# Two token streams staggered by half a tile at four layer norms of a two-layer flow backbone, and the adaLN vectors moved out of those norms

## The chip, the cores and the metric

The kernel runs on one core of a Trainium2 chip. The metric is the device time of one launch in microseconds (us), the median of several runs. TensorE (PE), VectorE (DVE), ScalarE (ACT) and GpSimd (POOL) each have a queue of instructions that they take in order; SyncE (SP) issues the DMA transfers.

## What is computed

The model has two layers over 512 tokens: 256 latent tokens and 256 context tokens, in 1024 channels. The two streams have the same weights and different adaLN vectors. Everything is fp32.

```python
for l in range(DEPTH):                       # DEPTH = 2
    mod = split(silu(c) @ ada_w[l] + ada_b[l], 9)        # latent; modc from c_ctx for the context
    h  = macaron_ffn(h,  mod[0],  mod[1],  mod[2],  ...) # hc likewise
    y, yc = token_mixer(modulate(h, mod[3], mod[4]), modulate(hc, modc[3], modc[4]), ...)
    h  = layer_norm(alpha * h + mod[5] * y)
    h  = macaron_ffn(h,  mod[6],  mod[7],  mod[8],  ...)
    # the last layer drops the context after the mixer
def macaron_ffn(h, shift, scale, gate, w_in, w_out, g, b):
    a, b = split(modulate(h, shift, scale) @ w_in, 2)
    return layer_norm(alpha * h + 0.5 * gate * ((silu(a) * b) @ w_out))
```

The mixer runs three branches (a gated recurrence, a long convolution, windowed attention), merges them with gates and applies one output projection. So there are six layer norms: after the FFN, the mixer and the FFN of each layer.

## The kernel before, in words

Channels lie on the 128 partitions, tokens along the free dimension: a tile is 128 channels by 512 tokens (latent 0 to 255, context 256 to 511). In the second layer the context is dropped behind the mixer's projections, so that later tiles have 256 tokens. Each weight is loaded in fp32 by SP into `raw` (`wload`, L120 to 132), split by ScalarE into a high part (L130) and by VectorE into the low rest (L132). A product is three matmuls in fp32r: high by high, high by low, low by high (`mm3`, L139 to 143; `projO`, L523 to 536). An FFN (`ffn`, L466) goes twice through eleven input blocks of two products (SwiGLU in `finish`, L474) and eight output products of eleven blocks each (L508 to 518), each added to the residual tile `ah` (`residual`, L361 to 380), which also sums the tiles and their squares for the norm. The mixer's output projection (L1132 to 1136) does the same with eight products.

`norm` (L391 to 455) then takes column sums with one-column matmuls (`token_mean`, L388 and 389), the mean over all partitions (L423), the variance (L424, L425), rstd by a pow on GpSimd (L426), spreads it over partitions (`bcast`, L457 to 462), and makes the eight operands of the next sub-layer: centre (L411), scale (L438), affine and cast (`mod`, L341 to 353), low part (`low`, L355 to 358). GpSimd writes the scaled residual back (L449). Its TensorE part is in a fixed order, behind the last product.

The adaLN vectors come in 18 groups of 512 columns a layer. They are made in three ways: the first four of layer 0 at the start; `ada_group` (L286 to 297) on TensorE, eight products of two stream columns by 512, in four column tiles, then four transposes and a sum; and `ada_pairs` (L250 to 284), which multiplies on VectorE (L266) weight by weight, for two groups and two streams a pair, and reduces on TensorE (L273). The latter is a generator: `pull` (L171 to 175) advances it by `BG` = (2, 1) steps behind each input block and each output product of an FFN, except in the first three slots. `run` (L1172 to 1194) says what goes where: three `ada_group`s inside each of the norms 0 to 3 (`HOLES` sets how many steps go between the norm's matmuls) and two in the fifth, four more in FFN slots (`fill`), and seven pairs (`bg`).

The order on each engine is made by a scheduler at build time, by program order and readiness; inside a `manual_schedule` block the named engines keep the written order, and `issue_after` puts an instruction behind another one. `U`, `T`, `E`, `H` and so on are pools of 128x512 slabs (`SLABS`), and `pj`, `ph`, `pa` are three, two and three PSUM banks (`BANKS`).

Of the kernel before, what the change touches and what calls it, by code (L numbers as in the profile page):

```python
# [27 lines left out]
PAIR0 = ((6, 7), (8, 9), (13, 14))  # L28
HOLES = (3, 0, 0, 2)
BG = (2, 1)  # L30
LAG = 4
SKIP = (1, 2, 3)
# [45 lines left out]
class Net:  # L78
    def __init__(self, ctx, tc, a, out):
        self.tc, self.nc, self.a, self.out = tc, tc.nc, a, out  # L80
        self.uid = 0
        self.now, self.chains = 0.0, []
        ep = lambda **k: ctx.enter_context(tc.tile_pool(**k))
# [50 lines left out]

    def split(self, src, hi, lo):
        self.nc.scalar.activation(hi, src, AF.Copy)
        self.nc.vector.tensor_tensor(lo, src, hi, ALU.subtract)
# [32 lines left out]

    def pull(self, n):  # L171
        self.slot += 1
        if self.slot not in self.bg_skip:
            for _ in range(n):
                next(self.bg, None)
# [74 lines left out]
    def ada_pairs(self, l, gs, mods):  # L250


        nc = self.nc
        for pair in gs:
            acc = []
            for g in pair:
                acc += [self.slab("W", name="acc") for _ in range(2)]
                for k in range(KD):
                    w = self.slab("EH"[k % 2], name="adaw")
                    nc.sync.dma_start(out=w, in_=self.a["ada_w"][l, g, k])  # L260
                    for t, s in zip(acc[-2:], range(2)):
# [5 lines left out]
                    if k % 2:  # L267
# [12 lines left out]
            v = tr.rearrange("p (b g s x) -> p g b s x", b=4, g=2, s=2)  # L280
            for i, g in enumerate(pair):
                bias = self.par("ada_b", l * 72 + g * 4, 4)
                nc.vector.tensor_tensor(mods[:, g * 4:g * 4 + 4, :], v[:, i, :, :, 0],
                                        bias.unsqueeze(2).to_broadcast([P, 4, 2]), ALU.add)
# [106 lines left out]
    def norm(self, l, i, ah, TT, st, mods_next, ish, keep=True, out=None, fill=()):  # L391
        nc = self.nc
        nb = TT // P
        units, end = [], None
        for f in fill:
            x = self.ada_group(*f)
            units += [(x, 1), end, (x, 1), (x, 1), (x, 1)] if end else [(x, 1)] * 4
            end = (x, 0)
        units += [end] if end else []

        def more(n):
            while units and n >= units[0][1]:
                x, m = units.pop(0)
                next(x, None)
                n -= m
# [8 lines left out]
        with self.tc.manual_schedule(engines={mybir.EngineType.PE}), self.tc.issue_after(self.last_mm.ins):  # L414
            more(HOLES[0])
            for tb in range(nb):
                self.token_mean(st["stat"][:, tb:tb + 1], st["s1"], tb, False, False)
            more(HOLES[1])
            for tb in range(nb):
                self.token_mean(st["stat"][:, 4 + tb:5 + tb], st["sq"], tb, False, tb == nb - 1)  # L420
            more(HOLES[2])
# [7 lines left out]
            more(HOLES[3])  # L429
            R = self.bcast(rstd, nb, "pa")  # L430
            more(100)
# [23 lines left out]
        return u + [self.low(x, TT) for x in pend]  # L455
# [10 lines left out]
    def ffn(self, l, i, u, ah, TT, gate, extra=None, pre=None):  # L466
# [4 lines left out]
        for half in range(2):  # L471
            g = []

            def finish(pa, pb):  # L474
                s = self.slab("T", name="silu")
                nc.scalar.activation(s[:, :TT], pa[:, :TT], AF.Silu)  # L476
                nc.vector.tensor_tensor(s[:, :TT], s[:, :TT], pb[:, :TT], ALU.mult)  # L477
                gh, gl = self.hilo(GTAGS[len(g)], "g")
                self.split(s[:, :TT], gh[:, :TT], gl[:, :TT])
                g.append((gh, gl))  # L480

            j = 0
            while j < HALF:
# [5 lines left out]
                if n == 3:  # L489
                    banks = self.projO(pre, u, [TT] * 6)  # L490
                elif n == 2:
                    banks = self.projO([w(q) for q in range(3)], u, [TT] * 3)
                    finish(*banks[:2])
                    banks = banks[2:] + self.projO([w(3)], u, [TT], "ph")
# [5 lines left out]
                self.pull(BG[0])  # L500
# [7 lines left out]
            for d in range(KD):  # L508
                if half and d == KD - 1:
                    self.squares(st, TT)  # L510
# [8 lines left out]
                self.pull(BG[1])  # L519
# [45 lines left out]
    def hgrn_proj(self, l, h, u, NQ, outer):  # L565
        nc = self.nc
        i = 4 + 4 * h
        if outer:
            ws = [self.wload(self.a["mix_w"][l, i + q], tags=(None, "QQ", "FF")[q],
                             marks=self.marks if q in PIN else None) for q in range(3)]  # L570
            pz = self.projO(ws, u, (T, T, NQ))
        else:
            pz = [self.projT(l, i + r, u, T) for r in range(2)]
        f, k = self.wide("F", name="f"), self.wide("F", name="k")
        for r in range(2):
            col = l * 8 + r * 4 + h
            c = slice(r * T, (r + 1) * T)
            nc.scalar.activation(f[:, c], pz[r], AF.Sigmoid)
            nc.scalar.activation(k[:, c], pz[r], AF.Sigmoid, scale=-1.0)
# [3 lines left out]
        pq = pz[2] if outer else self.projT(l, i + 2, u, NQ)  # L583
        q = self.slab("S", name="q")
        nc.scalar.activation(q[:, :NQ], pq[:, :NQ], AF.Copy)
        pg = self.projT(l, i + 3, u, NQ, "ph" if outer else "pj")
# [477 lines left out]
    def mixer(self, l, u, ah, TT, gate):  # L1064
# [31 lines left out]
        def proj(h):  # L1096
            hp.append(self.hgrn_proj(l, h, u, TT, h == 0))
# [34 lines left out]
        for d in range(KD):  # L1132
            if d == KD - 1:
                self.squares(st, TT)
# [4 lines left out]
    def run(self):  # L1139
# [21 lines left out]
        for d in range(KD):  # L1161
# [7 lines left out]
            if d < 2:  # L1169
# [4 lines left out]
                    [self.tables_b, lz(ada, 0, 15), lz(self.filters, 1)],  # L1174
            (1, 0): [None] + [lz(ada, 1, 15)],
        }
        bg = {(0, 0): self.ada_pairs(0, PAIR0, mods[0]),
              (0, 1): self.ada_pairs(1, [(1, 2), (3, 7)], mods[1]),
              (1, 0): self.ada_pairs(1, [(8, 9), (13, 14)], mods[1])}
        for l in range(DEPTH):  # L1180
            TT = T if l < DEPTH - 1 else L
            self.bg, self.slot, self.bg_skip = bg.get((l, 0), iter(())), 0, SKIP
            st = self.ffn(l, 0, u, ah, T, lambda: self.mod_cols(mods[l], 2), fill.get((l, 0)), pre if l == 0 else None)
            u = self.norm(l, 0, ah, T, st, mods[l], 3, fill=[(l, g, mods[l]) for g in (10, 11, 12)])
            st = self.mixer(l, u, ah, TT, self.mod_cols(mods[l], 5))
            u = self.norm(l, 1, ah, TT, st, mods[l], 6,
                          fill=[(l, 16, mods[l]), (l, 17, mods[l])] + ([(l + 1, 0, mods[l + 1])] if l < DEPTH - 1 else []))
            self.bg, self.slot, self.bg_skip = bg.get((l, 1), iter(())), 0, SKIP
            st = self.ffn(l, 1, u, ah, TT, lambda: self.mod_cols(mods[l], 8), fill.get((l, 1)))
            if l < DEPTH - 1:  # L1190
                u = self.norm(l, 2, ah, TT, st, mods[l + 1], 0, fill=[(l + 1, g, mods[l + 1]) for g in (4, 5, 6)])
            else:
                self.norm(l, 2, ah, TT, st, None, 0, out=self.out)
# [127 lines left out]
```

## Time and profile before

| | |
|---|---|
| median of 3 runs | 2384.67 us (2384.52 to 2386.96) |
| the profiled execution | 2383.82 us, span 2382.0 us |
| granted TensorE clock, mean | 0.994 |
| busy share: TensorE, its weight loads | 98%, 83% |
| busy share: VectorE, ScalarE, GpSimd | 60%, 41%, 7% |
| DMA | 360.41 MB, 151 GB/s |

The busy time of an engine counts whatever its instructions are for, so TensorE's 98% includes the column sums and adaLN products between sub-layers. A row of a timeline has the start, the busy time, engine, line, operation, the tiles written and read, the shape and the number of instructions merged; idle time before it, with what ended it, stands in brackets. An fp32 product appears as two records. A matmul's own time includes its way through the array, so the pace is read from starts.

### The profile page before, as it was taken

What the parts mean: (1) busy time and instruction counts of PE and PEld (TensorE: products, weight loads), DVE (VectorE), ACT (ScalarE), POOL (GpSimd) and SP (SyncE); (2) the same over time, 40 slices, a digit from 0 to 9 for tenths busy, and PEclk for the clock granted to TensorE, in tenths of its full rate; (3) what the DMA queues carried; (4) which work ended last, traced back from release to release, by engine and by line L of the source; (5) the groups of instructions that cost most, each with busy time, mean ns of one, the idle gap of its engine ahead of it and who ended that gap; (6) DMA issues with size and microseconds to landing.
All of it is one profiled execution on the core that took longest, in us unless ns stands there. A gap on an engine that the chain in (4) does not pass through costs nothing.

```text
span 2382.0 us, 34116 instructions
## 1 busy us (share of the span) xinstructions
PE 2343.4 (98%) x13112; PEld 1971.4 (83%) x13112; DVE 1440.5 (60%) x2403; ACT 970.3 (41%) x1663; POOL 170.3 (7%) x158
## 2 busy tenths in 40 slices
PE   8999999999999999999999999999999999999998
PEld 4778778699888888867888877878887999998998
DVE  3647848656877665776433357363346687776555
ACT  3424324444654433343222234222225466645443
POOL 1003002210010000010000001000002111000000
PEclk9999999999999999999999999999999999999999
DMA  9435734723223445765332247243224344694564
GB/s 365 139 102 172 233 97 121 263 67 105 77 80 128 154 137 190 254 207 156 108 121 93 83 139 251 90 149 106 92 86 137 118 129 138 197 320 153 171 198 125
DMA packets 153314, 360.41 MB, mean 151 GB/s; under 512 B 16576, under 2 KB 38208, under 8 KB 153152
## 3 DMA queue, kind: packets, MB, share of 16 engines
q1 hardware_dynamic: 153152, 358.24, 46.2%
q8 instruction: 103, 1.69, 0.3%
q14 instruction: 59, 0.48, 0.1%
HBM read 331.96 MB, written 26.21 MB: 150 GB/s over the span
## 4 chain that ended last, share of the span: by engine, by line
PE 94%; DMA 2%; DVE 2%; ACT 1%; issue 1%; SPq 1%; POOL 0%; ACTq 0%; DVEq 0%
PE pj L530 18%; PE pj L531 18%; PE pj L533 18%; PE pj L141 7%; PE pj L143 7%; PE pj L142 7%; PE ph L632 2%; PE pj L551 1%; PE pj L552 1%; PE pj L553 1%; PE ph L293 1%; PE pa L1006 1%; PE pa L873 1%; PE ph L678 1%; PE pa L997 1%
## 5 line engine op out<-in xcount | busy, mean ns | idle before, releaser
L132 DVE TENSOR_TENSOR lo<-raw,hi 128x1024 fp32r<-128x1024 f32 (+1 forms) x455 | 524.6, 1154 | 451.1 <-ACT hi L130 450.2
L530 PE MATMUL pj<-uh,hi 128*128 128x512 f32 (+1 forms) x2096 | 752.5, 359 | 4.6 <-ACT uh L352 3.0
L533 PE MATMUL pj<-ul,hi 128*128 128x512 f32 (+1 forms) x2096 | 749.2, 358 | 1.1 <-DVE ul L357 1.1
L531 PE MATMUL pj<-uh,lo 128*128 128x512 f32 (+1 forms) x2096 | 749.5, 358 | 0.0
L130 ACT ACTIVATE hi<-raw 128x1024 fp32r<-128x1024 f32 (+1 forms) x455 | 446.4, 982 | 602.3 <-issue 251.2
L530 PEld LDWEIGHTS pj<-uh,hi 128*128 128x128 f32 x2096 | 396.6, 189 | 74.5 <-issue 8.6
L533 PEld LDWEIGHTS pj<-ul,hi 128*128 128x128 f32 x2096 | 396.1, 189 | 59.3 <-DVE ul L357 2.5
L531 PEld LDWEIGHTS pj<-uh,lo 128*128 128x128 f32 x2096 | 396.4, 189 | 56.8 <-issue 2.1
L142 PE MATMUL pj<-g,hi 128*128 128x512 f32 (+1 forms) x704 | 255.7, 363 | 0.0
L143 PE MATMUL pj<-g,lo 128*128 128x512 f32 (+1 forms) x704 | 255.5, 363 | 0.0
L141 PE MATMUL pj<-g,hi 128*128 128x512 f32 (+1 forms) x704 | 255.4, 364 | 0.0
L141 PEld LDWEIGHTS pj<-g,hi 128*128 128x128 f32 x704 | 132.8, 189 | 23.7 <-issue 1.7
L143 PEld LDWEIGHTS pj<-g,lo 128*128 128x128 f32 x704 | 132.9, 189 | 22.3 <-DVE ah L366 1.7
L142 PEld LDWEIGHTS pj<-g,hi 128*128 128x128 f32 x704 | 132.9, 189 | 21.3 <-issue 0.8
L476 ACT ACTIVATE silu<-pj 128x512 f32<-128x512 f32 (+1 forms) x87 | 47.3, 543 | 244.2 <-PE pj L533 244.2
L266 DVE SCALAR_TENSOR_TENSOR acc<-adaw,sc,acc 128x512 f32<-128x512 f32 x196 | 138.2, 747 | 3.9 <-DMA adaw<-ada_w 3.5
L477 DVE TENSOR_TENSOR silu<-silu,pj 128x512 f32<-128x512 f32 (+1 forms) x83 | 51.3, 619 | 147.0 <-PE pj L533 135.7
L366 DVE SCALAR_TENSOR_TENSOR ah<-pj,hg,ah 128x256 f32<-128x256 f32 x136 | 60.3, 478 | 90.0 <-PE pj L143 70.3
L426 POOL TENSOR_TENSOR rstd<-var,mhalf 128x4 f32<-128x4 f32 (+1 forms) x6 | 6.4, 1063 | 1111.9 <-DVE var L425 1111.9
L551 PE MATMUL pj<-hi,uh 128*128 128x256 f32 x288 | 82.2, 288 | 0.2
L552 PE MATMUL pj<-lo,uh 128*128 128x256 f32 x288 | 81.9, 286 | 0.0
L553 PE MATMUL pj<-hi,ul 128*128 128x256 f32 x288 | 81.6, 286 | 0.0
(293 smaller groups left out, 3110.3 us busy)
## 6 DMA issues: line engine op xcount, KB each, us to landing
raw<-ffn_in SPq DMA_DIRECT2D x176, 512.0 KB, 3.4
adaw<-ada_w SPq DMA_DIRECT2D x256, 256.0 KB, 4.8
raw<-mix_w SPq DMA_DIRECT2D x124, 512.0 KB, 3.5
raw<-ffn_out SPq DMA_DIRECT2D x64, 384.0 KB, 3.1
raw<-ffn_out SPq DMA_DIRECT2D x64, 320.0 KB, 2.9
raw<-branch_w SPq DMA_DIRECT2D x24, 512.0 KB, 5.3
adaw<-ada_f SPq DMA_DIRECT2D x32, 256.0 KB, 6.0
raw<-out_w SPq DMA_DIRECT2D x16, 512.0 KB, 4.6
```

What stands on the lines that cost most here:

```text
L130: nc.scalar.activation(hi[:, :n], raw[:, :n], AF.Copy)
L132: nc.vector.tensor_tensor(lo[:, :n], raw[:, :n], hi[:, :n], ALU.subtract)
L141: nc.tensor.matmul(out, lhsT=wh, rhs=xh, start=start, stop=False)
L142: nc.tensor.matmul(out, lhsT=wh, rhs=xl, start=False, stop=False)
L143: self.last_mm = nc.tensor.matmul(out, lhsT=wl, rhs=xh, start=False, stop=stop)
L266: nc.vector.scalar_tensor_tensor(t, w, c, t, ALU.mult, ALU.add)
L530: self.nc.tensor.matmul(p, lhsT=hi, rhs=u[k][0][:, :n], start=(k == 0), stop=False)
L531: self.nc.tensor.matmul(p, lhsT=lo, rhs=u[k][0][:, :n], start=False, stop=False)
L533: self.last_mm = self.nc.tensor.matmul(p, lhsT=hi, rhs=u[k][1][:, :n], start=False, stop=(k == KD - 1))
L551: nc.tensor.matmul(o, lhsT=u[k][0][:, s], rhs=hi[:, c], start=(k == 0), stop=False)
L552: nc.tensor.matmul(o, lhsT=u[k][0][:, s], rhs=lo[:, c], start=False, stop=False)
L553: nc.tensor.matmul(o, lhsT=u[k][1][:, s], rhs=hi[:, c], start=False, stop=(k == KD - 1))
```

## The change

At norms 0, 1, 2 and 3 (both FFNs and the mixer of layer 0, and the first FFN of layer 1), `norm` gives way to `seam`. The last two output products of an FFN, or the last three of the mixer, are computed for the latent stream first and then for the context stream, in products of 256 columns; the latent stream's statistics, centring and rstd stand among the context stream's matmuls. Then the first three products of the next sub-layer run for the latent stream, with the context stream's statistics and centring among them, and then for the context stream. TensorE, VectorE and ScalarE all keep the written order in this block. The weights of those output products are split into slabs `U` (`wlast`); the fourth product of the next sub-layer follows with 512 columns.

The adaLN groups of those norms move: 10 and 11 of layer 0 into the first FFN's slots, 16 and 17 into the second's, 14 of layer 1 beside 15 into the third's; the others into `ada_pairs`, which has four parts in the first FFN, three in the second and three in the third (the last of them with four groups for the latent stream alone). `PULL` = (2.0, 1.0) replaces `BG`; in the second half an output product pulls one more, in the first half of the first FFN a half more. The filters of layer 1 move from the first FFN to the second. In the fifth norm the order of column sums and adaLN steps changes, and the groups' ends move behind the first products.

```diff
-PAIR0 = ((6, 7), (8, 9), (13, 14))
-HOLES = (3, 0, 0, 2)
-BG = (2, 1)
-SKIP = (1, 2, 3)
+SKIP = 3
+PULL = (2.0, 1.0)
+STATS = 5
+SEAM = {mybir.EngineType.PE, mybir.EngineType.DVE, mybir.EngineType.Activation}
...
+    def seam(self, l, prods, gate, ah, st, i, mods, ish, ws, ns):
...
+        def stats(s):
+            stat = self.pbank("pa")
+            x3 = (st["s2"], st["sq"][s], st["s1"])
+            for n, (x, o) in enumerate(zip(x3, (2, 2, 0))):
+                for tb in range(2):
+                    self.token_mean(stat[:, o + tb:o + tb + 1], x, (0 if n == 1 else 2 * s) + tb, n == 0 and tb == 0,
+                                    n == 2 and tb == 1)
+            mean[s] = self.pbank("pa")
+            nc.tensor.matmul(mean[s][:, :L], lhsT=self.onesD, rhs=st["s1"][:, cols(s)], start=True, stop=True)
...
+            nc.gpsimd.tensor_tensor(rstd[s][:, :2], var[:, :2], self.mhalf[:, :2], ALU.pow)
...
+        def operand(d, s):
...
+            nc.vector.tensor_tensor(t, t, R[s][:, :L], ALU.mult)
+            if d:
+                nc.scalar.activation(x[:, :L], t, AF.Identity, bias=b, scale=g)
+                h = nc.scalar.activation(uh[:, c], x[:, :L], AF.Copy)
...
+            w = nc.vector.tensor_tensor(ul[:, c], x[:, :L], uh[:, c], ALU.subtract)
...
+        with self.tc.manual_schedule(engines=SEAM), self.tc.issue_after(self.last_mm.ins):
+            banks = []
+            for s in range(2):
+                n = 0
+                for d, ops in prods:
+                    p = self.pbank("pj")
+                    for k, (wh, wl, xh, xl) in enumerate(ops):
+                        self.mm3(p[:, :L], wh, wl, xh[:, cols(s)], xl[:, cols(s)], k == 0, k == len(ops) - 1)
+                        n += s
+                        if n == STATS:
+                            stats(0)
+                        elif STATS < n <= STATS + KD:
+                            center(n - STATS - 1, 0)
+                        elif n == STATS + KD + 1:
+                            R[0] = self.bcast(rstd[0], 2, "pa")
+                    if not s or d < KD - 1:
+                        self.residual_of(d, p, gate, ah, st, s)
+                last = p
+            for s in range(2):
+                w = ws[:ns[s]]
...
+                for k in range(KD):
+                    if k < KD - 1:
+                        next(x[k + 1])
+                    next(x[k])
...
+                    if not s:
+                        if k == 0:
+                            self.residual_of(KD - 1, last, gate, ah, st, 1)
+                        elif k == 2:
+                            stats(1)
+                        elif 2 < k < KD - 1:
+                            center(2 * k - 6, 1)
+                            center(2 * k - 5, 1)
+                        if k == 5:
+                            R[1] = self.bcast(rstd[1], 2, "pa")
...
-                self.pull(BG[1])
+                if d == 3 and half:
+                    for _ in self.bg:
+                        pass
+                elif d < 3 or not half:
+                    self.pull(PULL[1] + (1.0 if half else 0.5 if pre else 0.0))
...
-                    [self.tables_b, lz(ada, 0, 15), lz(self.filters, 1)],
-            (1, 0): [None] + [lz(ada, 1, 15)],
+                    [self.tables_b, lz(ada, 0, 10), lz(ada, 0, 11)],
+            (1, 0): [None] * 10 + [lz(ada, 1, 14), lz(ada, 1, 15)],
+            (0, 1): [None] * 3 + [lz(ada, 0, 16), lz(ada, 0, 17), None, lz(self.filters, 1)],
...
-        bg = {(0, 0): self.ada_pairs(0, PAIR0, mods[0]),
-              (0, 1): self.ada_pairs(1, [(1, 2), (3, 7)], mods[1]),
-              (1, 0): self.ada_pairs(1, [(8, 9), (13, 14)], mods[1])}
+        bg = {(0, 0): (0, [(6, 7), (8, 9), (12, 15), (13, 14)]),
+              (0, 1): (1, [(0, 1), (2, 3), (4, 5)]),
+              (1, 0): (1, [(6, 7), (8, 9), (10, 11, 12, 13)])}
...
-            u = self.norm(l, 0, ah, T, st, mods[l], 3, fill=[(l, g, mods[l]) for g in (10, 11, 12)])
...
-                          fill=[(l, 16, mods[l]), (l, 17, mods[l])] + ([(l + 1, 0, mods[l + 1])] if l < DEPTH - 1 else []))
...
-                u = self.norm(l, 2, ah, TT, st, mods[l + 1], 0, fill=[(l + 1, g, mods[l + 1]) for g in (4, 5, 6)])
```

## Rows read from the trace of the kernel before

**Rows 1.** The page: busy shares of the engines, and the chain's shares.
```profile
PE 2343.4 (98%) x13112; PEld 1971.4 (83%) x13112; DVE 1440.5 (60%) x2403; ACT 970.3 (41%) x1663; POOL 170.3 (7%) x158
...
PE 94%; DMA 2%; DVE 2%; ACT 1%; issue 1%; SPq 1%; POOL 0%; ACTq 0%; DVEq 0%
```

**Rows 2.** Stages: start:end, us, PE, PEld, DVE, ACT, POOL busy, clock, DMA.
```profile
60.00:441.50 381.50, 381.49 (x1715) 301.62 (x1713) 253.16 (x378) 140.86 (x204) 46.60 (x37) 1.00 0.49 156
441.50:462.06 20.56, 16.57 (x92) 7.34 (x91) 12.99 (x23) 7.97 (x13) 5.05 (x5) 0.83 0.83 298
1034.40:1051.22 16.82, 14.31 (x92) 6.23 (x91) 11.28 (x21) 8.15 (x14) 3.39 (x5) 0.90 0.96 321
...
1419.80:1434.87 15.07, 13.65 (x91) 6.31 (x90) 11.64 (x22) 8.21 (x14) 3.32 (x4) 1.00 0.97 339
1434.90:1803.00 368.10, 368.10 (x1634) 299.37 (x1632) 174.64 (x248) 111.26 (x152) 6.83 (x5) 1.00 0.39 125
1803.00:1818.07 15.07, 13.65 (x92) 6.32 (x91) 11.84 (x22) 6.89 (x12) 3.32 (x4) 1.00 0.81 278
2166.80:2178.00 11.20, 8.59 (x61) 3.96 (x59) 8.64 (x21) 6.20 (x11) 2.94 (x6) 1.00 0.65 194
```

**Rows 3.** Timeline of TensorE through the third norm's stretch and just behind it.
```profile
1420.90 1.05 PE L389 MATMUL pa<-onesD,sq 128*128 128x1 f32 x8
...
1425.52 1.10 PE L423 MATMUL pa<-S,onesD 128*128 128x512 f32 x2
...
1428.33 0.66 PE L321 MATMUL ph<-prm,ada 128*128 128x128 f32 x4 [0.71 <-ACT ada L318]
1428.83 1.06 PE L461 MATMUL pa<-prm,rstd 128*128 128x128 f32 x8
1429.81 1.92 PE L293 MATMUL ph<-adaw,sc 128*32 128x512 f32 x16
...
1438.44 0.60 PE L321 MATMUL ph<-prm,ada 128*128 128x128 f32 x4
```

**Rows 4.** Timeline of TensorE in the first norm's stretch.
```profile
453.27 2.08 PE L461 MATMUL pa<-prm,rstd 128*128 128x128 f32 x8 [2.58 <-POOL rstd L426]
455.28 3.64 PE L293 MATMUL ph<-adaw,sc 128*32 128x512 f32 x16
```

**Rows 5.** Timeline of TensorE in the fifth norm: the mean of 256 columns.
```profile
2170.08 0.68 PE L423 MATMUL pa<-S,onesD 128*128 128x256 f32 x2
```

**Rows 6.** Timeline of TensorE: products of 512 columns, and of 256 columns.
```profile
100.22 0.39 PE L530 MATMUL pj<-uh,hi 128*128 128x512 f32 x1
...
100.90 0.39 PE L530 MATMUL pj<-uh,hi 128*128 128x512 f32 x1
...
2249.85 0.28 PE L141 MATMUL pj<-g,hi 128*128 128x256 f32 x1
...
2250.21 0.28 PE L141 MATMUL pj<-g,hi 128*128 128x256 f32 x1
```

**Rows 7.** Timelines of VectorE and ScalarE at the fifth norm, operations of 256 columns.
```profile
2179.51 0.41 DVE L411 TENSOR_TENSOR t<-ah,pa 128x256 f32<-128x256 f32 x1
2179.84 0.42 DVE L357 TENSOR_TENSOR ul<-u,uh 128x256 fp32r<-128x256 f32 x1
...
2178.02 0.59 ACT L350 ACTIVATE u<-t,B,G 128x256 f32<-128x256 f32 x1
...
2178.97 0.59 ACT L350 ACTIVATE u<-t,B,G 128x256 f32<-128x256 f32 x1
```

**Rows 8.** Groups by line and shape on VectorE, first FFN (60 to 441.5 us).
```profile
L266 DVE SCALAR_TENSOR_TENSOR acc<-adaw,sc,acc 128x512 f32<-128x512 f32 x84 | 58.8, 744 | 3.5 <-DMA adaw<-ada_w 3.5
L132 DVE TENSOR_TENSOR lo<-raw,hi 128x1024 fp32r<-128x1024 f32 x39 | 48.7, 1250 | 40.3 <-ACT hi L130 40.3
L132 DVE TENSOR_TENSOR lo<-raw,hi 128x768 fp32r<-128x768 f32 x16 | 16.5, 1031 | 0.2 <-ACT hi L130 0.2
```

**Rows 9.** Timeline of TensorE in the third FFN: the reduction of a pair.
```profile
1557.92 1.06 PE L273 MATMUL ph<-acc,ones 128*32 128x512 f32 x8
```

More of the change, by code (lines that the diff above doesn't have):

```diff
@@ L1 @@
+import itertools
 import math
@@ L169, in drain, with begin @@
             self.step(c)
+    def begin(self, bg):
+        self.bg, self.slot, self.due = bg, 0, 0.0
     def pull(self, n):
         self.slot += 1
-        if self.slot not in self.bg_skip:
-            for _ in range(n):
-                next(self.bg, None)
+        if self.slot <= SKIP:
+            return
+        self.due += n
+        while self.due >= 1.0:
+            self.due -= 1.0
+            next(self.bg, None)
     def setup(self):
@@ L253, in ada_pairs @@
         nc = self.nc
-        for pair in gs:
+        for part in gs:
+            ns = 4 // len(part)
             acc = []
-            for g in pair:
-                acc += [self.slab("W", name="acc") for _ in range(2)]
+            for g in part:
+                acc += [self.slab("W", name="acc") for _ in range(ns)]
                 for k in range(KD):
@@ L393, in norm @@
         nb = TT // P
[L394 to L399, printed above, removed]
-        def more(n):
[L402 to L405, printed above, removed]
+        groups = [[self.ada_group(*f), KD // 2] for f in fill]
+        def more(n):
+            for x in groups:
+                while n and x[1]:
+                    next(x[0])
+                    x[1] -= 1
+                    n -= 1
         c = []
@@ L414, in norm @@
         with self.tc.manual_schedule(engines={mybir.EngineType.PE}), self.tc.issue_after(self.last_mm.ins):
[L415 to L421, printed above, removed]
+            self.squares(st, TT)
+            more(2)
+            for x, o, e in ((st["sq"], 4, True), (st["s1"], 0, False)):
+                for tb in range(nb):
+                    self.token_mean(st["stat"][:, o + tb:o + tb + 1], x, tb, False, not e and tb == nb - 1)
             stat, st["mean"] = st["stat"], self.pbank("pa")
@@ L457, in bcast, with end_groups @@
+    def end_groups(self):
+        for x in self.ends:
+            next(x, None)
+        self.ends = []
     def bcast(self, cols, nb, tag):
@@ L490, in ffn @@
                     banks = self.projO(pre, u, [TT] * 6)
+                elif n == 2 and heads:
+                    banks = [list(x) for x in zip(*heads)]
+                    w3 = self.wload(a["ffn_in"][l, i, jj + 1, 1], tags="FF", marks=self.marks)
+                    with self.tc.issue_after(self.behind.ins):
+                        finish(*banks[:2])
+                    banks = banks[2:] + self.projO([w3], u, [TT], "pa")
                 elif n == 2:
@@ L508, in ffn @@
             for d in range(KD):
-                if half and d == KD - 1:
-                    self.squares(st, TT)
+                if half and seam and d == KD - 2:
+                    prods = []
+                    for dd in (d, d + 1):
+                        w = []
+                        for k0, k1 in ((0, 6), (6, HALF)):
+                            w += self.wlast(a["ffn_out"][l, i, half, dd][:, k0 * P:k1 * P], k1 - k0)
+                        prods.append((dd, [(*w[k], *g[k]) for k in range(HALF)]))
+                    return self.seam(l, prods, hg, ah, st, **seam)
                 p = self.pbank("pj")
@@ L1062, in merge, with mixer @@
         return res
-    def mixer(self, l, u, ah, TT, gate):
+    def mixer(self, l, u, heads, ah, TT, gate, seam):
         nc = self.nc
@@ new lines, in run @@
+            r = self.mixer(l, u, heads, ah, TT, self.mod_cols(mods[l], 5),
+                           None if last else dict(i=1, mods=mods[l], ish=6, **ffn_head(l, 1)))
+            u, heads = r if not last else (self.norm(l, 1, ah, TT, r, mods[l], 6, fill=[(l, g, mods[l]) for g in (16, 17)]),
+                                           None)
+            background(l, 1)
+            r = self.ffn(l, 1, u, ah, TT, lambda: self.mod_cols(mods[l], 8), fill.get((l, 1)), None, heads,
+                         None if last else dict(i=2, mods=mods[l + 1], ish=0, **ffn_head(l + 1, 0)))
@@ L1192, in run @@
+            if last:
+                self.norm(l, 2, ah, TT, r, None, 0, out=self.out)
             else:
-                self.norm(l, 2, ah, TT, st, None, 0, out=self.out)
+                u, heads = r
 def _cols(v):
```

158 lines of the change are left out of this document (124 added, 34 removed).

## The prediction

> **What bounds the kernel now.** I read the page's engine shares and its chain first [rows 1]: TensorE is busy for 98% of the span and makes up 94% of the chain that ended last, so only what leaves or enters TensorE's queue counts, plus waits of TensorE itself. Then the stages [rows 2]: inside the FFNs TensorE has no gap at all (381.49 of 381.50 us, 368.10 of 368.10 us), while VectorE is busy for 66% of the first FFN and 47% of the third. What is not products lies in the stretches between the last product of one sub-layer and the first product of the next: 20.6, 16.8, 15.1 and 15.1 us at the four norms that the change rewrites, **67.5 us** together, and 11.2 us at the fifth. They are nearly full of TensorE work, so "busy" hides them; the third view, TensorE in order of time through the third of these stretches, tells what it does there [rows 3]: 24 column sums of one column (eight in 1.0 us), the mean (two records, 1.0 us), the broadcast of rstd (eight, 1.0 us) and, in between, three adaLN groups of 16 records (1.9 us each) with their transposes. These groups fill the wait for the normalisation; they are not bound to this place.
>
> A side note on the first stretch: there TensorE waited 2.58 us for rstd, and the broadcast and the adaLN records behind it ran at twice the usual length (2.08 us for eight, 3.64 us for sixteen) [rows 4], with a mean granted clock of 0.83 over the stretch, 0.90 in the second and 1.00 in the others [rows 2]; so part of it is at the lower of the two levels (1.2 rather than 2.4 GHz). That is why those two stretches are longer, and it goes with them.
>
> **The change part by part.**
>
> *Removed:* the four stretches as they are, -67.5 us.
>
> *What comes back of the norms:* the column sums are as many as before, 24 records at 1.0/8 us = 3.0 us; the mean becomes two products of 256 columns, 0.6 us each (the row of the fifth norm, which has 256 columns [rows 5]: two records for one product); the broadcast stays at 1.0 us. 5.2 us a norm, **+20.6 us** in all with the decimals of the rows.
>
> *Splitting:* products of 512 columns start every 0.68/3 = 0.227 us, those of 256 every 0.36/3 = 0.120 us [rows 6], each with its own weight load in both cases; one product split in two costs 2 x 0.120 - 0.227 = 0.013 us. Two output products of an FFN are 2 x 11 x 3 = 66 matmuls, the three of the mixer 72, and the three first products behind a norm 72 (48 at the fourth, where the third of them has 256 columns anyway): 138 + 144 + 138 + 114 = 534, **+7.1 us**. The Trainium skill says otherwise (TensorE: Matmul & The Clock Gate, section Back-to-back issue gap): a warm matmul starts N/2.4 + 2.5 ns after the one before, which would make a split cost 2.5 ns, the term 1.3 us and the time some 6 us lower. No row here is that fast at either width, so the sum keeps the rows' figure.
>
> *Waits inside a seam.* No run of before shows one, so I bound it. Lowest: nothing, and not below, since the work on TensorE is counted whole. Highest: the serial chain shown by the third stretch, from the end of the mean at 1426.6 to the first product at 1434.9, 8.2 us each [rows 2, 3]. In between, I set the new order against 256-column operations at the fifth norm [rows 7]: VectorE starts one every 0.33 us, ScalarE needs 0.95 us for an affine and a cast in sequence. The first stream's chain has 17 steps of three matmuls as cover in an FFN (6.1 us; 19 in the mixer), and its pow on GpSimd (1 to 2 us) and its centring fit. Then TensorE takes 9 x 0.12 = 1.08 us per step of the first stream's new products; VectorE needs 0.67 us for scaling and low part, and 1.34 us in the four steps that also centre two tiles of the other stream: it falls behind by 4 x 0.26, and with the ramp at either stream's start I take 1.3 us. At the fourth norm the second stream has two weights only, 0.72 us a step against ScalarE's 0.95: eight steps make that seam 3.0 us. The weight of the fourth product is split on ScalarE and then VectorE (there 1.25 us [rows 8]) in the middle of the second stream; queued behind it are operands that TensorE waits for, with some 1 us of lead: 0.5 us each. Together 3 x 1.3 + 3.0 + 4 x 0.5 = **+8.9 us**, nearer to nothing than to 33 because each step's queue has more time than work on average.
>
> *Moved onto TensorE in the FFNs:* eight groups are now made there instead of four, so four more at 1.9 us and 0.5 us of transposes [rows 3]: **+9.6 us**. Their copy on ScalarE, for which the transposes waited 0.71 us in the stretch, is hidden by products.
>
> *Moved onto VectorE:* ten parts instead of seven, each with eight matmul records, 1.0 us [rows 9], and 0.5 us of transposes: **+4.5 us** on TensorE. On VectorE they are 3 x 28 = 84 more operations, at 58.8/84 = 0.70 us [rows 8] 59 us, one part in each of three FFNs. Cover: VectorE's free 128 us of the first FFN and 193 us of the third [rows 2]; the filters of layer 1 leave the first FFN for the second. The pull rate per pair of input products stays two and leaves room: of 48 x 0.227 = 10.9 us VectorE has eight adaLN products (5.6 us), two weight splits (2.5 us [rows 8]) and two operations of 512 columns (1.3 us at twice the pitch of 256), 9.4 us. Between the first FFN's first eight output products the rate rises from one to 1.5: 4.2 us, splits of some 1.0 us each [rows 8] and a residual of 0.7 to 0.9, 7.1 of 33 x 0.227 = 7.5 us, tight but inside. Without cover each part would cost its 20 us. I take 0.
>
> *Queues passed:* the loads of twelve groups (eight of 256 KB each) leave stretches where the DMA engines are 81 to 97% busy for FFNs at 39 to 49% [rows 2]; on SP they stand among the FFN's weight loads, which have products of 10.9 us a pair as cover. GpSimd scales each tile in two halves instead of one, with 5 us of work in a 20 us stretch [rows 2]. Nothing for either; if SP's queue blocked a weight, TensorE would wait in an FFN, which today it never does.
>
> *Small:* the third group's transposes behind each stretch (0.4 us [rows 3]) go, **-1.5 us**. At the fifth norm both groups' transposes move behind the first products; of its 2.6 us without TensorE work (11.20 - 8.59 [rows 2]) I take half, **-1.3 us**.
>
> Sum: -67.5 + 20.6 + 7.1 + 8.9 + 9.6 + 4.5 - 1.5 - 1.3 = **-19.6 us**. The profiled execution took 2383.82 us (span 2382.0); the median of the runs is 0.85 us above it, so on the median the forecast is 2384.67 - 19.6 = **2365 us**.
>
> **The rivals.** (A) *Waits of 5 us a seam.* All three engines run in written order, so one late item (a weight that has not been split, rstd behind GpSimd's scalings) holds everything behind it. For it: in the first stretch rstd alone cost 2.58 us [rows 4]. Against it: cover of 6.1 us. 4 x 5 us instead of 8.9 gives 2376 us.
>
> (B) *The staggering hides nothing:* the change does not do what it says, and each seam keeps the serial 8.2 us and 1.3 us more for feeding, 38 us in place of 8.9. Time: 2394 us in full; with three quarters of the chain open, 4 x (6.2 + 1.3) = 30 us, 2386 us, no change. I take the latter: the other stream's matmuls cannot all be missed. For it: in the third stretch that chain is 8.2 us long although three engines are free for it. Against it: 17 steps, 6.1 us, stand beside it in the written order.
>
> (C) *VectorE becomes the bound in the FFNs.* Its place is the SwiGLU product and the low parts of the weights, queued behind the adaLN products; its price is up to 59 us, 2424 us if nothing of the added work is covered. The change is slower than today by over 0.2% (2389.4 us) from 24.4 us on, when 41% of the 59 us lies open; with half of it open the time is 2395 us. For it: 95% between output products. Against it: 66% and 47% busy, and not one gap of TensorE at the same pull rate.
>
> **How the numbers follow.** A measurement of this kernel tells 0.2%, 4.8 us, from no change. The forecast gets 0.67, A 0.16 (both faster), B 0.09 (the same), C 0.08 (slower), which makes 0.83, 0.09 and 0.08. Low end: no waits in the seams and all 2.6 us of the fifth norm, 2365 - 8.9 - 1.3 = 2354.8, so 2354. High end: A with its spread, 2379; beyond it lie B and C, 17%.
>
> **What would show it.** Between the last product before each of the four norms and the first after it no stretch without products longer than some 2 us; L293 only inside FFNs and at the fifth norm; granted clock 1.00 in the former first and second stretch; TensorE's starts 0.120 us apart in the seams; its waits there for VectorE's low part or ScalarE's cast of 1 to 3 us a norm; VectorE some 59 us busier, and TensorE still without gaps in the FFNs. It is wrong if the seams show waits over 3 us each (A, B), or if the FFNs show waits for VectorE (C).

## The result, and the profile after

The changed kernel takes **2373.0 us** (median of 5 runs, 2372.65 to 2373.56) beside 2384.96 us of the kernel before on the same chip (5 runs, 2384.52 to 2386.96): a ratio of 0.9949, 95% interval 0.9934 to 0.9964, or 12.0 us less. The forecast was 2365 us, in a range of 2354 to 2379: the sign and the range held, and about 8 us of the gain are missing.

The profiled execution has a span of 2370.7 us, 11.3 less than before. Its page opens with the engines' busy time, which answers to the first row of [rows 1]:

```profile
PE 2327.8 (98%) x13530; PEld 1996.5 (84%) x13530; DVE 1502.0 (63%) x2610; ACT 989.9 (42%) x1743; POOL 181.9 (8%) x194
```

TensorE has 418 records more and is busy for 15.6 us less; VectorE is busy for 61.5 us more, as forecast (59). Neither tells where the time went. That comes from the starts of the stages, read off TensorE's timelines of both kernels:

| from the first product of ... to ... | before, us | after, us | difference |
|---|---|---|---|
| start of the span to the mixer of layer 0 | 462.06 | 444.74 | -17.3 |
| mixer of layer 0 to the second FFN | 589.2 | 583.2 | -6.0 |
| second FFN to the third (the filters of layer 1 moved in) | 383.7 | 392.5 | +8.9 |
| third FFN to the mixer of layer 1 | 383.2 | 377.8 | -5.4 |
| mixer of layer 1 to its last product (second half of a seam) | 348.7 | 356.6 | +7.8 |
| fifth norm | 11.2 | 12.4 | +1.2 |
| from there to the end | 204.0 | 203.4 | -0.6 |

Two of these rows vary by themselves. Of the first row's 17.3 us, 1.6 lie ahead of ScalarE's first SwiGLU operation (66.46 us instead of 68.04), and the kernels built from the changed one have it anywhere from 66.46 to 68.46. The mixer of layer 1 varies by 2.6 us among kernels that are alike there.

The four stretches of [rows 2] are gone. This is TensorE's timeline through the first seam; the rows left out are products at the same pace:

```profile
436.43 0.95 PE L417 MATMUL pa<-onesD,sq 128*128 128x1 f32 x8
437.24 0.58 PE L417 MATMUL pa<-onesD,S 128*128 128x1 f32 x4
437.69 0.68 PE L502 MATMUL pa<-S,onesD 128*128 128x256 f32 x2
...
441.43 0.60 PE L605 MATMUL pa<-prm,rstd 128*128 128x128 f32 x4
...
444.50 0.28 PE L161 MATMUL pj<-g,wh 128*128 128x256 f32 x1
444.62 0.28 PE L162 MATMUL pj<-g,wl 128*128 128x256 f32 x1
444.74 0.28 PE L565 MATMUL pj<-uh,hi 128*128 128x256 f32 x1
```

Sums, mean and broadcast of the latent stream stand among the context stream's output products, products follow one another every 0.12 us, and the first product of the mixer starts 0.12 us after the last of the FFN. What was 20.6 us there [rows 2] is no gap at all. So the missing gain is elsewhere; TensorE's waits of the whole run, summed by the waiting line and its releaser (us in total, times, longest), name it:

```profile
PE ph L301 <- DVE acc L294: 8.3, 3, 5.4
...
PE pa L605 <- POOL rstd L449: 3.3, 2, 2.6
...
PE pj L565 <- ACT uh L522: 1.8, 2, 1.2
```

L301 (L273 before) is the reduction on TensorE of a part that VectorE summed (L294). The kernel before had no such wait. It lies in the first FFN, behind the first input products of its second half:

```profile
263.41 0.39 PE L702 MATMUL pj<-ul,hi 128*128 128x512 f32 x1
264.65 1.04 PE L301 MATMUL ph<-acc,ones 128*32 128x512 f32 x2 [0.85 <-DVE acc L294]
267.77 1.05 PE L301 MATMUL ph<-acc,ones 128*32 128x512 f32 x2 [2.08 <-DVE acc L294]
274.21 3.24 PE L301 MATMUL ph<-acc,ones 128*32 128x512 f32 x4 [5.39 <-DVE acc L294]
278.13 1.11 PE L307 MATMUL ph<-prm,ada 128*128 128x128 f32 x4 [0.69 <-ACT ada L304]
278.90 0.78 PE L699 MATMUL pj<-uh,hi 128*128 128x512 f32 x1
279.47 0.63 PE L700 MATMUL pj<-uh,lo 128*128 128x512 f32 x1
279.90 0.63 PE L702 MATMUL pj<-ul,hi 128*128 128x512 f32 x1
```

For 15 us no product runs, and the ones behind start 0.43 us apart, not 0.227 [rows 6], at the lower granted clock (0.50 from 278.90 to 282.46 us). VectorE's timeline shows why the sums were late:

```profile
243.66 1.23 DVE L134 TENSOR_TENSOR lo<-raw,hi 128x1024 fp32r<-128x1024 f32 x1 [4.01 <-ACT hi L132]
248.44 3.40 DVE L294 SCALAR_TENSOR_TENSOR acc<-adaw,sc,acc 128x512 f32<-128x512 f32 x5 [3.56 <-DMA adaw<-ada_w]
...
270.10 8.89 DVE L294 SCALAR_TENSOR_TENSOR acc<-adaw,sc,acc 128x512 f32<-128x512 f32 x13
```

From 103 to 248 us VectorE runs not one adaLN product; it even idles for 3.56 us, for an `adaw` tile that has not landed. Then the sums come in a burst, with VectorE busy for 15.15 of the 15.26 us without products, while TensorE's queue had the reduction at 264.65. Before, the burst was as late, and the reduction stood in four pairs of records among products, without a wait:

```profile
250.03 3.40 DVE L266 SCALAR_TENSOR_TENSOR acc<-adaw,sc,acc 128x512 f32<-128x512 f32 x5 [3.54 <-DMA adaw<-ada_w]
...
270.78 1.04 PE L273 MATMUL ph<-acc,ones 128*32 128x512 f32 x2
...
272.65 1.04 PE L273 MATMUL ph<-acc,ones 128*32 128x512 f32 x2
...
279.29 1.04 PE L273 MATMUL ph<-acc,ones 128*32 128x512 f32 x2
...
282.09 1.05 PE L273 MATMUL ph<-acc,ones 128*32 128x512 f32 x2
```

The changed kernel has all eight records in one block behind the product at 263.41, so the first pair stands 6 us earlier than before and the last some 17 us (1.6 us of both come from the earlier start).

By stretches (start:end, us, PE, PEld, DVE, ACT, POOL busy, clock, DMA): the second half of the first FFN's input products, its output products up to the mixer, a stretch of the second FFN, one of the third, and the fifth norm, in the columns of [rows 2]:

```profile
236.44:380.12 143.68, 134.68 (x594) 103.60 (x592) 97.41 (x142) 42.28 (x57) 2.12 (x2) 0.95 0.58 192
380.12:444.74 64.62, 64.62 (x361) 55.61 (x360) 36.92 (x72) 21.99 (x36) 1.69 (x3) 1.00 0.37 110
...
1060.00:1400.00 340.00, 340.00 (x1537) 276.56 (x1536) 212.80 (x317) 115.67 (x164) 21.97 (x17) 1.00 0.50 163
1450.00:1780.00 330.00, 330.00 (x1485) 268.69 (x1484) 157.41 (x229) 98.15 (x134) 0.00 (x0) 1.00 0.42 134
2154.84:2167.26 12.42, 8.89 (x57) 3.56 (x55) 9.56 (x21) 7.31 (x14) 3.82 (x6) 0.86 0.56 171
```

The first row holds 9.0 us without TensorE work, at a clock of 0.95. The stretches of the second and third FFN have no gap, with VectorE at 63% and 48%.

### The profile page after: what moved, and what is told of

Same layout as the page of the kernel before. It is cut to its first block, busy times and chain, and to the rows that moved or that the text cites. A ratio compares the mean times of both kernels' runs of the same rounds, so it can differ in the third digit from the quotient of the medians.

```text
span 2370.7 us, 35242 instructions
## 1 busy us (share of the span) xinstructions
PE 2327.8 (98%) x13530; PEld 1996.5 (84%) x13530; DVE 1502.0 (63%) x2610; ACT 989.9 (42%) x1743; POOL 181.9 (8%) x194
## 5 line engine op out<-in xcount | busy, mean ns | idle before, releaser
L134 DVE TENSOR_TENSOR lo<-raw,hi 128x1024 fp32r<-128x1024 f32 (+2 forms) x444 | 517.6, 1167 | 382.3 <-ACT hi L132 380.0
L699 PE MATMUL pj<-uh,hi 128*128 128x512 f32 (+1 forms) x2064 | 740.6, 359 | 2.8 <-ACT uh L380 2.8
L700 PE MATMUL pj<-uh,lo 128*128 128x512 f32 (+1 forms) x2064 | 738.0, 358 | 0.0
L702 PE MATMUL pj<-ul,hi 128*128 128x512 f32 (+1 forms) x2064 | 736.4, 358 | 0.0
L132 ACT ACTIVATE hi<-raw 128x1024 fp32r<-128x1024 f32 (+2 forms) x444 | 437.5, 987 | 562.6 <-issue 235.8
L161 PE MATMUL pj<-g,hi 128*128 128x512 f32 (+1 forms) x638 | 229.9, 361 | 0.0
L160 PE MATMUL pj<-g,hi 128*128 128x512 f32 (+1 forms) x638 | 229.9, 361 | 0.0
L162 PE MATMUL pj<-g,lo 128*128 128x512 f32 (+1 forms) x638 | 229.8, 360 | 0.0
L294 DVE SCALAR_TENSOR_TENSOR acc<-adaw,sc,acc 128x512 f32<-128x512 f32 x280 | 194.6, 745 | 10.6 <-DMA adaw<-ada_w 9.6
L160 PEld LDWEIGHTS pj<-g,hi 128*128 128x128 f32 x638 | 120.4, 189 | 20.4 <-ACT hi L132 1.7
L161 PEld LDWEIGHTS pj<-g,hi 128*128 128x128 f32 x638 | 120.5, 189 | 18.7 <-issue 0.8
L162 PEld LDWEIGHTS pj<-g,lo 128*128 128x128 f32 x638 | 120.6, 189 | 17.9
```

Of the source, the lines that this page charges most:

```text
L132: nc.scalar.activation(hi[:, :n], raw[:, :n], AF.Copy)
L134: nc.vector.tensor_tensor(lo[:, :n], raw[:, :n], hi[:, :n], ALU.subtract)
L160: nc.tensor.matmul(out, lhsT=wh, rhs=xh, start=start, stop=False)
L161: nc.tensor.matmul(out, lhsT=wh, rhs=xl, start=False, stop=False)
L162: self.last_mm = nc.tensor.matmul(out, lhsT=wl, rhs=xh, start=False, stop=stop)
L699: self.nc.tensor.matmul(p, lhsT=hi, rhs=u[k][0][:, :n], start=(k == 0), stop=False)
```

## The experiments

Two theories stood against each other for the missing 8 us. **Order:** the parts of the first FFN cost because the reduction is placed in TensorE's queue ahead of sums that come late, and any edit that takes one of the two away gives the time back. **Load:** VectorE has too little time in the FFNs, so that other placements only move the wait. Runs 1 to 3 change one thing each; 4 to 6 take the change apart; 7 to 10 go to the fifth norm.

**1. The rate of the first half undone** (in the changed kernel):

```diff
-                    self.pull(PULL[1] + (1.0 if half else 0.5 if pre else 0.0))
+                    self.pull(PULL[1] + (1.0 if half else 0.0))
```

> Theory (the pull rate of 1.5 between the first eight output products puts the reduction of the second VectorE part ahead of its sums, and TensorE waits 8.3 us there and runs some 3 us at the lower clock): at a rate of one the waits of L301 in the first FFN fall below 2 us and the time falls by 7 to 10 us, to 2363 to 2366. Rival (the sums are late because their weights are, held up by the slabs and transfers of the filters, whatever the rate): the wait stays at 6 us or more and the time within 2 us of 2373.

Measured: 2363.32 us (2359.74 to 2365.95), ratio to the kernel before 0.9903 (0.9889 to 0.9916): 9.7 us less than the changed kernel, with intervals apart. No row of L301 waiting for VectorE is left among TensorE's waits, and the second half's input products read:

```profile
238.16:369.98 131.82, 131.82 (x594) 101.78 (x592) 96.59 (x142) 42.16 (x57) 1.96 (x2) 1.00 0.65 209
```

The same 594 records, no gap, and clock 1.00 instead of 0.95. They take 11.9 us less; as they begin 1.7 us later here (the first SwiGLU is as much later), they end 10.1 us earlier, at 369.98 instead of 380.12 us. The span is 10.6 us shorter: nearly the whole difference is in this place.

**2. The reduction two steps later:**

```diff
-LAG = 4
+LAG = 6
```

> The changed kernel, its pull rate of 1.5 kept, with six empty steps between a part's last product on VectorE and its reduction on TensorE (LAG 6 for 4). Theory (TensorE waits because the reduction stands ahead of sums that VectorE has not made): two steps are 10 us of output products, more than the 8.3 us waited, so the waits of L301 in the first FFN fall below 2 us and the time to 2363 to 2366, as with the lower rate. Rival (the rate itself loads VectorE or the DMA queue so much that something else waits): waits of L301 or others stay above 5 us, 2370 or more.

Measured: 2364.55 us (2363.21 to 2367.04), ratio 0.9913 (0.9899 to 0.9926), and no wait of L301. Not one VectorE operation was taken away; only the place of the reduction changed. It stands in four pairs again, the first at 269.60 us and the last at 280.91.

**3. The filters of layer 0 five slots later:**

```diff
-F0, F1 = 3, 7
+F0, F1 = 8, 2
```

> The changed kernel, its pull rate kept, with the filters of layer 0 five input blocks later (F0, F1 = 8, 2), behind the first FFN's first output products. Theory (the filters hold the slabs into which the adaLN weights are loaded, so the sums of the second part start in a burst, behind time): the part's sums are made evenly and its reduction waits below 2 us; 2363 to 2366, unless a later part meets the filters instead (then a wait of the same 5 to 9 us stands there). Rival (the slabs have no part in it): the wait of 8 us stays where it is.

Measured: 2364.7 us (2359.51 to 2367.24), ratio 0.9911 (0.9896 to 0.9925), no wait of L301. The filters take their tiles from the pools `E` and `H`, where `adaw` lies too (L287). With them moved away VectorE's timeline has adaLN products where there were none; the second part's begin at 170.27 us instead of 248.44:

```profile
170.27 6.05 DVE L294 SCALAR_TENSOR_TENSOR acc<-adaw,sc,acc 128x512 f32<-128x512 f32 x9
...
238.98 2.07 DVE L294 SCALAR_TENSOR_TENSOR acc<-adaw,sc,acc 128x512 f32<-128x512 f32 x3
```

The reduction is earlier still (its first pair at 193.86 us) and yet waits for nothing. So the wait needs both: sums held up by the filters, and a reduction pulled forward by the half step a product. What of the filters holds the sums up was moved as one: their slabs, their VectorE work and their place among SP's transfers. The slabs are the likely part, but no run tells them apart. Order it is; each of three unlike edits gives back 8 to 10 us.

**4. The move alone, without staggering** (in the kernel before: the adaLN groups, parts, rates and filters placed as in the change, and the four norms left with nothing to fill them):

```diff
-SKIP = (1, 2, 3)
+SKIP = 3
+PULL = (2.0, 1.0)
...
-            u = self.norm(l, 0, ah, T, st, mods[l], 3, fill=[(l, g, mods[l]) for g in (10, 11, 12)])
+            u = self.norm(l, 0, ah, T, st, mods[l], 3)
```

> The kernel before with the adaLN groups moved as in the change, and the four norms as they were, without adaLN steps in them; nothing is staggered. Theory (the staggering, not the move, is what gains): each stretch keeps 4 us of statistics and a chain of 8.2 us, part of it at the lower clock, 12 to 15 us, against some 8 us that a seam costs; 2389 to 2400, slower than the kernel before. Rival (taking the adaLN steps out of the stretches is the gain by itself): 2373 or less.

Measured: 2394.79 us (2390.36 to 2397.88), ratio 1.0034 (1.0021 to 1.0048): slower than before. Its four stretches:

```profile
443.35:455.26 11.91, 6.08 (x35) 4.72 (x33) 9.46 (x16) 4.53 (x7) 3.34 (x4) 0.70 0.55 191
1031.50:1043.12 11.62, 7.15 (x35) 5.17 (x33) 9.26 (x15) 4.53 (x7) 3.30 (x4) 0.65 0.51 156
1429.86:1442.10 12.24, 6.50 (x36) 4.73 (x34) 9.90 (x16) 4.53 (x7) 3.31 (x4) 0.69 0.47 162
1814.30:1826.62 12.32, 7.79 (x35) 6.20 (x34) 9.58 (x16) 4.53 (x7) 3.31 (x4) 0.72 0.55 174
```

They fall from 67.5 to 48.1 us, 20.6 us of them without TensorE work, at a granted clock of 0.65 to 0.72. The moved work and the reductions' waits, 8.2 us here too, cost more than the 19.4 us gained; that sum was not taken apart. So the staggering is worth 2394.79 - 2373.0 = 21.8 us by the medians and some 20 by the ratios, and the move pays only because the seams need no filling. Some 12 of them are read directly (48.1 us of stretches against the 36 us that the seams cost, below); the rest was not placed. The run's mean clock is 0.984, that of the changed kernel 0.994.

**5. The latent stream's statistics eight steps later:**

```diff
-STATS = 5
+STATS = 13
```

> The first stream's statistics stand eight steps later in each seam (STATS 13 for 5), so nine steps of output products (3.2 us) are left as cover for rstd, broadcast and first operand instead of seventeen. Theory (those steps are what hides the chain): TensorE waits some 1 to 1.5 us more at each of the four seams, 4 to 6 us in all, 2377 to 2379. Rival (cover to spare, the chain is far shorter than 3 us): no change over 1 us.

Measured: 2376.98 us (2374.74 to 2378.93), ratio 0.9961 (0.9947 to 0.9974), 4.0 us more than the changed kernel by the medians, 2.9 by the ratios. The intervals overlap, but the waits show a row that the changed kernel doesn't have, beside one that both have:

```profile
PE pj L565 <- ACT uh L524: 4.3, 4, 1.1
...
PE pj L565 <- ACT uh L522: 1.8, 2, 1.3
```

Four waits, one at each seam's first new product. The 17 steps ahead of it are cover that is used: with 9 left it begins to fail, by about 1 us a seam.

**6. VectorE loaded further** (in the kernel of run 1: each VectorE product of the layer-1 parts done twice, the second time with a factor of zero, 168 operations more):

```diff
+                            if l:
+                                nc.vector.scalar_tensor_tensor(t, w, self.sc[:, k, 2:3], t, ALU.mult, ALU.add)
```

> The kernel with the pull rate of one, and in the second and third FFN every adaLN product on VectorE made twice, the second time with a factor of zero: 168 more operations of 0.70 us, 118 us. Theory (VectorE's work is covered as long as a part's sums are there before its reduction): four pairs of input products with loads each overrun by 4 us (15.0 of 10.9 us), and the two pairs without loads give 14 of the 16 us back, so TensorE waits 2 to 12 us in all at L301 and the time is 2365 to 2375. Rival (VectorE is the bound of these FFNs): a quarter or more of the 118 us shows, 2393 or more.

Measured: 2377.14 us (2374.42 to 2377.8), ratio 0.9962 (0.9948 to 0.9976): 13.8 us more than run 1, just above the range of the one theory and far below the time of the other. The group of the added operations, by line (count, busy us, mean ns, idle before):

```profile
L296 DVE SCALAR_TENSOR_TENSOR acc<-adaw,sc,acc 128x512 f32<-128x512 f32 x168 | 119.9, 744 | 0.1
```

So 88% of 119.9 us was covered, and the waits at the reductions that the theory expected did not come. What did come through is partly seen. The adaLN products of layer 1 do not stay in the FFNs: in this run and in run 1 they already stand at 930 us, in the mixer, where VectorE's residual and low parts are waited for. The window 960 to 1030 us has TensorE busy for 65.51 us instead of 69.75 at a clock of 0.95 instead of 1.00, and among TensorE's waits in it are two that run 1 lacks:

```profile
PE pj L701 <- DVE ah L396: 2.4, 1, 2.4
PE pj L702 <- DVE lo L134: 1.6, 1, 1.6
```

That stage of the mixer, its output products up to the second FFN, is 54.2 us long instead of 46.7, some half of the 13.8 us. Most of the rest lies in the second FFN (129.0 instead of 123.0 us for the input products of its second half), in the columns of [rows 2]:

```profile
1231.66:1360.90 129.24, 127.98 (x553) 100.54 (x552) 125.74 (x184) 40.60 (x53) 0.00 (x0) 1.00 0.52 164
```

There VectorE is busy for 125.74 of 129.24 us (87.10 of 123.22 in run 1). So VectorE is not the bound of the changed kernel, but this much more work fills it in one stage, and that stage grows.

**7. The fifth norm in its old order** (in the changed kernel; the adaLN steps, their ends and the column sums ordered as before):

```diff
...
+            more(3)
             self.squares(st, TT)
-            more(2)
-            for x, o, e in ((st["sq"], 4, True), (st["s1"], 0, False)):
+            for x, o, e in ((st["s1"], 0, False), (st["sq"], 4, True)):
...
-        self.ends = [x for x, _ in groups]
```

> Only the fifth norm has its column sums and adaLN steps in the order of before. Theory (the new order there lets TensorE reach the broadcast 2.6 us before rstd is there, and then run sixteen records at the lower clock): the stretch of the fifth norm shrinks from 12.4 to about 11.2 us and the time by 1 to 2.5 us. Rival (the stretch is bound by the chain of column sums, rstd and operands in either order): no change over 0.5 us.

Measured: 2374.08 us (2371.17 to 2376.0), ratio 0.9949 (0.9936 to 0.9963): no change, where the theory had 1 to 2.5 us. The stretch is 12.6 us with the old order too, and its timeline says why:

```profile
2162.24 0.71 PE L607 MATMUL pa<-prm,rstd 128*128 128x128 f32 x4 [1.11 <-POOL rstd L452]
2162.88 3.38 PE L321 MATMUL ph<-adaw,sc 128*32 128x512 f32 x12
```

In the kernel before the same two rows are:

```profile
2174.32 0.71 PE L461 MATMUL pa<-prm,rstd 128*128 128x128 f32 x4 [1.20 <-POOL rstd L426]
2174.96 1.91 PE L293 MATMUL ph<-adaw,sc 128*32 128x512 f32 x12
```

The same twelve records take 1.91 us there, in a stretch at clock 1.00 [rows 2]. The order and the waits are alike, and the clock falls in one and not in the other. Ahead of the stretch TensorE was busy for 94% of some 25 us in both, at a mean clock of 0.93 here and 1.00 before. What decides it is open.

**8 to 10. The wait of the fifth norm filled, the variance hoisted, and both** (in the kernel of run 1):

```diff
-            nc.scalar.activation(msq[:, :nb], stat[:, :nb], AF.Square)
...
+            with self.tc.high_priority(offset=HOIST):
+                nc.scalar.activation(msq[:, :nb], stat[:, :nb], AF.Square)
...
-            more(2)
+            more(6)
             R = self.bcast(rstd, nb, "pa")
```

Run 8 has both edits, run 9 `more(6)` alone, run 10 the hoist alone.

> The kernel with the pull rate of one, with six adaLN steps instead of two ahead of the broadcast at the fifth norm (24 records), and the three small operations behind the column sums ahead of weight splits in the queues of ScalarE and VectorE. Theory (at the fifth norm TensorE runs out of work for 2.6 us, drops to the lower clock, and is then held up by its own sixteen records while the first operand is ready): the wait for rstd shrinks below 1 us, the records run at 1.9 us for sixteen, the stretch falls from 12.4 to 9 to 10.5 us and the time to 2360 to 2362. Rival (the chain through VectorE and ScalarE bounds it): no change over 0.5 us against 2363.3.

> The kernel with the lower pull rate, with six adaLN steps instead of two ahead of the broadcast at the fifth norm and nothing hoisted. Theory (the gain of the filled fifth norm is the filling: four more steps, 16 records, stand where TensorE waited 2.59 us for rstd): 2358 to 2361 us, as with both edits (2358.85 us), the stretch at the fifth norm some 10.5 to 11 us. Rival (the hoisted variance and pow are what gives it): 2362 to 2365 us, as without either edit (2363.32 us).

> The kernel with the lower pull rate, with two adaLN steps ahead of the broadcast as before, and the norm's variance and pow hoisted ahead of the centring. Theory (the filling gives it): 2361 to 2364 us, with a wait for rstd that is shorter by at most 1 us. Rival (the hoisting gives it): 2358 to 2360 us, with no wait for rstd over 0.5 us at the fifth norm.

Measured: 2358.85 us (2357.55 to 2359.46), ratio 0.9887 (0.9874 to 0.9900), with both; 2361.37 (2359.0 to 2363.48), 0.9903 (0.9888 to 0.9917), filled; 2360.75 (2360.13 to 2364.32), 0.9904 (0.9888 to 0.9921), hoisted. The medians do not tell the last two from each other, nor from run 1 (0.9903), and none of the three lies in the range that its theory gave. The traces tell them apart. The changed kernel, from the mean on:

```profile
2158.45 0.68 PE L446 MATMUL pa<-S,onesD 128*128 128x256 f32 x2
2159.05 1.06 PE L321 MATMUL ph<-adaw,sc 128*32 128x512 f32 x8
2162.71 0.74 PE L605 MATMUL pa<-prm,rstd 128*128 128x128 f32 x4 [2.59 <-POOL rstd L449]
2163.38 3.53 PE L321 MATMUL ph<-adaw,sc 128*32 128x512 f32 x16
```

Filled alone:

```profile
2149.40 0.68 PE L446 MATMUL pa<-S,onesD 128*128 128x256 f32 x2
2150.01 2.78 PE L321 MATMUL ph<-adaw,sc 128*32 128x512 f32 x24
...
2153.67 0.71 PE L605 MATMUL pa<-prm,rstd 128*128 128x128 f32 x4 [0.29 <-POOL rstd L449]
```

Hoisted alone:

```profile
2146.60 1.07 PE L321 MATMUL ph<-adaw,sc 128*32 128x512 f32 x8
2150.26 0.71 PE L606 MATMUL pa<-prm,rstd 128*128 128x128 f32 x4 [2.59 <-POOL rstd L450]
2150.90 3.62 PE L321 MATMUL ph<-adaw,sc 128*32 128x512 f32 x16
```

Hoisting leaves the wait at 2.59 us to the digit. Filling takes it to 0.29 and keeps the higher clock (granted 1.00 there): 24 records in 2.78 us, where 8 and 16 took 1.06 and 3.53 (the sixteen at 0.53). Behind them TensorE then waits 1.51 us for the first operand, a wait that the slow records had covered. From the mean to the first product it is 8.8 us in run 1 and hoisted, 6.9 filled and with both. So the filling is worth 1.9 us in this place, the hoist nothing that a trace shows. In the whole run the filling alone is not seen: the span is 2359.7 us, in run 1 2360.1, as the mixer of layer 1, which the edit leaves alone, takes 2.6 us longer (357.4 us instead of 354.8). From the first product to the end the filled kernels have 203.4 us and run 1 204.3, but the changed kernel has 203.4 without filling. The lower median of the run with both has no further cause that I found. At 2358.85 us it beats both kernels of the case by the medians, 25.8 us under the kernel before.

## Why the prediction came out as it did

*Removed stretches, -67.5 us:* held. No seam has a gap like those.

*Statistics that come back, +20.6 us:* too high. Twelve column sums, a mean and a broadcast take 2.2 us a stream in the seams, 17.7 us in all.

*Splitting, +7.1 us:* the pace held, 0.120 us between starts throughout the seams. The shorter gap of the Trainium skill (TensorE: Matmul & The Clock Gate, Back-to-back issue gap), 256/2.4 + 2.5 = 109 ns, is the pace of no run here (0.119 us at the least over twenty starts), so the rows were the right choice. The section gives it for an isolated matmul; the prediction applied it to a stream of weight loads and matmuls.

*Waits in the seams, +8.9 us:* somewhat low. Between products of 256 columns, without those right behind column sums, mean and broadcast, starts later than 0.12 us add up to 2.0, 2.0, 2.0 and 5.0 us at the four norms, 11.0 us in all, with the fourth the longest, as expected from its two weights. Rival A (5 us each) fell at three of the four; run 5 shows that the cover is real and how far it goes. Rival B (the staggering hides nothing) fell to run 4.

*Moved onto TensorE, +9.6, and the parts' share of it, +4.5:* not separated by a run; nothing speaks against them.

*Moved onto VectorE, "I take 0":* **this step failed.** It set VectorE's work against the time of a product, average against average ("7.1 of 7.5 us, tight but inside"), and never asked at which point of TensorE's queue the reduction would stand and when its sums would be ready. The half step more a product moved the reduction forward by 6 us and more, to 264.65 us, while the sums stayed where the filters let them begin, at 248.44. The wait was 8.3 us; with the slower products behind it the first FFN lost 10.3 to 11.9 us from its first SwiGLU to the mixer (against runs 1 to 3). The term should have been +10 to +12, not 0. Rival C had the engine pair right and the mechanism wrong: VectorE's share was not the limit (runs 2 and 3 have the same work and no wait), the order was.

*The fifth norm, -1.3 us:* it came to +1.2. I took half of the time without TensorE work as gained; instead of two waits of 0.71 and 1.20 us there is one of 2.59, another 0.94 us are waited for squares that twelve adaLN records had covered, and the sixteen records behind it ran at the lower clock (3.53 us; 12 took 1.91 before). But run 7 shows that the old order is as long in this neighbourhood, so this loss isn't the edit's alone.

Together, with 11 us for the failed step: -19.6 - 2.9 + 2.1 + 11 + 2.5 = -6.9 us, against -11.3 between the two spans, of which 1.6 lie ahead of the first SwiGLU; some 3 us of gain have no term. With the failed step undone (run 1) the kernel takes 2363.3 us, 1.7 below the forecast.

## What to carry to other kernels

When work moves from a stall to a background stream, its consumer's place in the in-order queue matters more than the producer's load: compare when the last operand is ready with where the consumer stands, and look for what else holds the buffers of the first load. Staggering two independent halves by one stage pays when the cover is counted in steps (here 17 products of three matmuls, 6.1 us, for a chain that took 8.2 us before), and then the filler that used to sit in the stall can go where it has slack. Where a wait can't be removed, it can be filled with work that is due anyway: at the fifth norm sixteen records kept the higher clock that way and 1.9 us were gained, less than the wait shrank, because the next operand was then waited for.

## What was not expected of the hardware

The granted clock behind a wait of one to three microseconds is not settled by the wait. After 2.59 us TensorE ran sixteen records in 3.53 and 3.62 us (changed kernel and run 10, granted clock 0.53); after 1.11 us (run 7) twelve took 3.38 at 0.54, and after 1.20 us (before) the same twelve took 1.91 at 1.00. VectorE could take 119.9 us more at 0.74 us an operation, and the kernel lost 13.8.
